# The second weight chunk ahead of the low-rank gate's weights, and a gate product stacked in 96 rows

## The chip, the cores and the metric

The kernel runs on one core of a Trainium2 chip. The metric is the device time of one execution in microseconds (us), as the median of several runs. One core has five engines with a queue each: TensorE (PE, with its weight loads shown as PEld), VectorE (DVE), ScalarE (ACT), GpSimd (POOL) and SyncE (SP), which here only issues transfers. The transfers themselves run on 16 DMA engines.

## The reference

One decoder layer on 256 tokens of 1024 channels in float32: a mixer (gated linear attention beside causal pooling, merged and projected), then a mixture of 64 experts. What matters here is the start of the mixer, where x meets one wide input projection, and the gate of the attention, which has rank 16:

```python
proj = jnp.einsum('bsd,de->bse', x, w_in)          # columns: q 512, k 512, v 1024, r 1024, g_lr 16, u 512, gates 2048
log_decay = jax.nn.log_sigmoid(
    jnp.einsum('bsr,rk->bsk', g_lr, w_gate_up) + b_gate) / GLA_GATE_TEMP     # w_gate_up: 16 x 512
```

## The kernel before, in words

The order of every engine's instructions is the order in which the program writes them (`tc.manual_schedule()`), so an instruction that waits holds all later ones of its engine.

**Precision.** TensorE multiplies float32r data in one pass. To keep float32 accuracy an operand is split in two float32r parts, hi (ACT copies, L295) and lo (DVE subtracts, L296). A product then takes three matmuls: hi by hi, hi by lo, lo by hi (`mm3`, L299 to L301). Plain float32 operands take more passes.

**The input projection.** The weights `w_in` come in chunks of 256 columns, 1 MB each, through a ring of eight buffers that SP fills (`Ring.issue`, L64 to L87). The list `pieces` (L623 to L632) says in which order chunks are worked off: the first chunk of q in four parts with x coming in between, then the gate's piece ("g"), then the second chunk of q in two parts, then k, v and so on. `run` (L305) writes the split of a piece two pieces ahead of its matmuls. After each piece a step of the attention (`gla_steps`, L358) is written in between.

**The low-rank gate.** Its first product is `rank_mm` (L614): 16 matmuls of `wgs` (the hi and lo parts of the 16 columns side by side, 32 columns) with x hi and x lo into `pg`, 32 rows by 256 tokens; ACT copies these to `glr` as float32 (L621). The second product (L362 to L368) multiplies `glr` with `wgu`, in which `w_gate_up` stands twice, one below the other, in plain float32: four matmuls into `plog`. DVE then adds the bias.

**SP's queue at the start** (L256 to L272): x and the first chunk in turns, `wg` (the 16 gate columns), `wgu` as two transfers, `b_gate`, the second chunk (L261), `cst1` (192 KB of constants, L262), the rest of `cst` (L263), five more chunks, then small vectors and the router's weights.

**POOL's queue at the start**: `identb` from `ident` (L278), `trib` from `cst1` (L279), then the zeroing of `A0` and `A1` (L344, L345) and of `B` (L372).

**Later.** After the mixer come the router and 16 rounds of four experts; their matrices stream through rings whose buffers come free when TensorE has used them.

Of the kernel before, what the change touches and what calls it, by code (L numbers as in the profile page):

```python
# [5 lines left out]
FT = mybir.dt.float32  # L6
FR = mybir.dt.float32r
BF = mybir.dt.bfloat16
I32 = mybir.dt.int32
AF = mybir.ActivationFunctionType  # L10
# [3 lines left out]
T, D = 256, 1024  # L14
# [8 lines left out]
NR1, NR2, NR3 = 8, 6, 5  # L23
# [86 lines left out]
def body(ctx, tc, A, out, dbg=lambda *a: None, stop=None):  # L110
    nc = tc.nc
    ctx.enter_context(tc.manual_schedule())
    PE, V, S, G = nc.tensor, nc.vector, nc.scalar, nc.gpsimd
# [74 lines left out]
    ring = Ring(nc, loads)  # L188
# [6 lines left out]
    def bank(tag, shape, name):  # L195
        t = psum.tile([128, 512], FT, name=name, tag=tag, bufs=4)
        n = 1
        for s in shape:
            n *= s
        v = t[:, :n]  # L200
        if len(shape) == 2:
            v = v.rearrange("p (a b) -> p a b", b=shape[1])
        elif len(shape) == 3:
            v = v.rearrange("p (a b c) -> p a b c", b=shape[1], c=shape[2])
        return v
# [23 lines left out]
    ring1 = ctx.enter_context(tc.tile_pool(name="ring1", bufs=NR1))  # L229
# [4 lines left out]
    gla = tc.alloc_tile_pool(name="gla", bufs=1)  # L234
# [8 lines left out]

    x = ring1.tile([128, 2048], FT, name="x", tag="w1", bufs=NR1).rearrange("p (t d) -> p t d", t=2)
    wg = gla.tile([128, 8, 16], FT, name="wg")
    wgu = gla.tile([32, 512], FT, name="wgu")
    wgrp = right.tile([128, 4, 128], FT, name="wgrp")
    nc.scalar.dma_start(ident, A["cst"][:, C_ID:C_ID + 128])
    halves = [slice(0, 512), slice(512, 1024)]
# [5 lines left out]
    ring.between = load_x  # L255
    ring.issue(ring1, "w1", NR1)  # L256
    nc.sync.dma_start(wg, w_in[:, 3072:3088].rearrange("(k p) c -> p k c", p=128))
    for n in range(2):
        nc.sync.dma_start(wgu[16 * n:16 * n + 16], A["w_gate_up"][0])
    nc.sync.dma_start(bgate, A["b_gate"][0].rearrange("(h p) -> p h", p=128))  # L260
    ring.issue(ring1, "w1", NR1)  # L261
    nc.sync.dma_start(cst1, A["cst"][:, C_KEPT:])  # L262
    nc.sync.dma_start(cst[:, C_IOTA:], A["cst"][:, C_IOTA:C_KEPT])  # L263
    ring.open(ring1, "w1", NR1, first=3)
# [6 lines left out]
                                     ap=[[0, 128], [1, E]]))  # L271
# [22 lines left out]
    def split_to(src, hi, lo, eng=V):  # L294
        S.activation(hi, src, AF.Copy)  # L295
        eng.tensor_sub(lo, src, hi.bitcast(FT))  # L296
# [18 lines left out]
    xTh = xt.tile([128, 8, T], FR, name="xTh", tag="xTh", bufs=1)  # L315
    xTl = xt.tile([128, 8, T], FR, name="xTl", tag="xTl", bufs=1)
    def x_part(c):
        p = bank("b", (2, T), "xp")
        for kk in range(2):
            for t in range(2):  # L320
                k = 2 * c + kk
                PE.transpose(p[:, kk, 128 * t:128 * (t + 1)], x[:, t, 128 * k:128 * (k + 1)], ident)
        ks = slice(2 * c, 2 * c + 2)
        split_to(p, xTh[:, ks], xTl[:, ks])


    p = bank("a", (128,), "warm")
# [8 lines left out]

    qT = gla.tile([128, H, T], FT, name="qT")
    kT = gla.tile([128, H, T], FT, name="kT")
    glr = gla.tile([32, T], FT, name="glr")
    wgs = gla.tile([128, 8, 2, 16], FR, name="wgs")  # L340
    v = right.tile([128, 2, D], FT, name="v")
    A0 = right.tile([128, H, 256], FT, name="A0")
    A1 = right.tile([128, H, 128], FT, name="A1")
# [14 lines left out]
    def gla_steps():  # L358
        yield
        xb = gla.tile([128, H, T], FT, name="E", bufs=2)  # L360
        for hp in range(2):
            p = bank("b", (2, T), "plog")  # L362
            for h2 in range(2):
                h = 2 * hp + h2
                PE.matmul(p[:, h2], wgu[:, 128 * h:128 * (h + 1)], glr, start=True, stop=True)
            for h2 in range(2):
                h = 2 * hp + h2
                V.tensor_scalar(xb[:, h], p[:, h2], bgate[:, h:h + 1], None, op0=OP.add)  # L368
# [64 lines left out]
        while m <= 128:  # L433
# [21 lines left out]
            if m < 128:  # L455
                n = H * T // (2 * m)
# [117 lines left out]
    def proj_piece(name, c, part, parts, st):  # L574
        i, kn = li[name, c], 8 // parts

        def sp():
            st[part] = split(ring.get(i)[:, kn * part:kn * (part + 1)], 256 * kn)
            if part == parts - 1:
                ring.done(i)  # L580

        def mm():
            if part == 0:
                st["p"] = bank("a", (2, T), "proj")
            p = st["p"]
            h, l = st[part]
            for j in range(2):
                for kk in range(kn):
                    k = kn * part + kk
                    first, last = k == 0 and j == 0, k == 7  # L590
                    if name == "v":
                        ts = slice(128 * j, 128 * (j + 1))
                        mm3(p[:, j], xTh[:, k, ts], xTl[:, k, ts], h[:, kk], l[:, kk], first, last, True)
                    else:
                        cs = slice(128 * j, 128 * (j + 1))
                        mm3(p[:, j], h[:, kk, cs], l[:, kk, cs], xTh[:, k], xTl[:, k], first, last, True)
            if part < parts - 1:
                return
            cs = slice(2 * c, 2 * c + 2)
            if name == "q":  # L600
                S.activation(qT[:, cs], p, AF.Copy, scale=DK ** -0.5)
            elif name == "k":
                V.tensor_copy(kT[:, cs], p)
            elif name == "v":
                V.tensor_copy(v[:, :, 256 * c:256 * (c + 1)], p)
            elif name == "u":
                V.tensor_copy(uT[:, cs], p)
            elif name == "r":
                S.activation(rT[:, cs], p, AF.Copy)
            else:  # L610
                S.activation(rows(GA if name == "ga" else GB, 2 * c, 2), p, AF.Copy)
        return sp, mm

    def rank_mm():  # L614
        pg = bank("b", (T,), "pg")

        for k in range(8):
            w = wgs[:, k].rearrange("p a r -> p (a r)")
            PE.matmul(pg[:32], w, xTh[:, k], start=k == 0, stop=False)
            PE.matmul(pg[:32], w, xTl[:, k], start=False, stop=k == 7)  # L620
        S.activation(glr, pg[:32], AF.Copy)  # L621

    pieces = []  # L623
    for name, c, _ in chunk_cols:
        st = {}
        parts = 4 if (name, c) == ("q", 0) else 2
        for part in range(parts):
            if parts == 4 and part < 3:
                pieces.append((("x", part, True), lambda: None, lambda part=part: x_part(part + 1)))
            pieces.append(((name, c, part == parts - 1),) + proj_piece(name, c, part, parts, st))  # L630
        if (name, c) == ("q", 0):
            pieces.append((("g", 0, 1), lambda: split_to(wg, wgs[:, :, 0], wgs[:, :, 1]), rank_mm))  # L632

    def done(key):
        finished.add(key)
# [3 lines left out]
    def chain(*gens):  # L639
        for g in gens:  # L640
            yield from g

    finished = {None}
    bgs = [dict(gen=pool_steps(), need=("u", 1)),
           dict(gen=chain(gla_steps(), out_steps(), done("out"), gate_steps()), need=("g", 0))]

    def step_bg():
# [536 lines left out]
    for q in range(NQ):  # L1184
# [34 lines left out]
        if q == SH_UP:  # L1219
            p = bank("b", (2, T), "shu")  # L1220
# [110 lines left out]
```

## Time and profile before

| what | value |
|---|---|
| median of three runs | 690.24 us (690.22 to 690.63) |
| profiled execution, its own time | 690.94 us |
| span of that execution, first to last instruction | 689.1 us |
| mean granted TensorE clock | 0.994 of full speed |

Times in the rows below are in us from the start of the span unless marked ns. An arrow in brackets after a row says how long the engine sat idle before it and what ended that.

### The profile page before, as it was taken

Reading aid. Unit: us, or ns where it says so; the run is one execution under the profiler, and the core shown is the slowest. Engines: PE = TensorE matmul, PEld = TensorE weight load, DVE = VectorE, ACT = ScalarE, POOL = GpSimd, SP = SyncE. Lnnn points to the kernel's source line nnn. Section 1 sums busy time; section 2 is a strip of 40 time slices with the busy share of each in tenths; the row PEclk is TensorE's granted clock in tenths of the full one; section 3 lists DMA queues with packets and bytes.
Section 4 is the critical chain, followed back from the end, with each engine's and each line's share of the span. In section 5 each row is a group of like instructions: output and inputs, shape, how many; then the busy total and the mean of one; then the engine's idle time right before and its main releaser. Section 6 shows DMA issues by size and latency. Waiting matters only on the chain. (4 is left out here: it accounts for less than half of the span.)

```text
span 689.1 us, 13639 instructions
## 1 busy us (share of the span) xinstructions
PE 667.2 (97%) x5928; PEld 472.6 (69%) x5928; DVE 289.3 (42%) x458; ACT 227.9 (33%) x348; POOL 66.2 (10%) x53
## 2 busy tenths in 40 slices
PE   8999999999999999999999999999999999799994
PEld 7999999999999756556556546556655665464632
DVE  4699845946676522122123123333431321231216
ACT  5554546674445213123123113221311311131122
POOL 1063404600002000000000002100000000100001
PEclk9999999999999999999999999999999999999997
DMA  8995533499677999999999999999999999999991
GB/s 265 302 349 185 182 123 126 148 384 421 248 260 300 352 422 384 421 420 418 419 421 419 421 418 416 405 419 421 419 419 421 419 420 420 420 421 416 407 332 63
DMA packets 67429, 242.02 MB, mean 351 GB/s; under 512 B 7044, under 2 KB 37508, under 8 KB 43560
## 3 DMA queue, kind: packets, MB, share of 16 engines
q1 hardware_dynamic: 67224, 241.07, 89.2%
q8 instruction: 47, 0.77, 0.5%
q10 hardware_dynamic: 144, 0.07, 0.1%
q14 instruction: 14, 0.11, 0.0%
HBM read 240.07 MB, written 1.05 MB: 350 GB/s over the span
## 5 line engine op out<-in xcount | busy, mean ns | idle before, releaser
L1032 PE MATMUL pgu<-w,xg 128*64 128x256 f32 x1840 | 222.4, 381 | 1.0 <-DMA w<-in_w_exp_gate 1.0
L1032 PEld LDWEIGHTS pgu<-w,xg 128*64 128x64 f32 x1840 | 140.3, 137 | 84.1 <-ACT Y L1062 11.7
L1057 PE MATMUL py<-w,ht 128*32 128x512 f32 (+1 forms) x912 | 119.3, 580 | 1.9 <-DMA w<-in_w_exp_down 1.5
L296 DVE TENSOR_TENSOR sl<-w,sh 128x1024 fp32r<-128x1024 f32 (+1 forms) x63 | 83.4, 1329 | 42.5 <-ACT sh L295 42.2
L1039 DVE TENSOR_TENSOR h<-sg,pgu 128x256 f32<-128x256 f32 x32 | 13.5, 422 | 192.5 <-ACT sg L1038 146.9
L1063 DVE SCALAR_TENSOR_TENSOR Y<-py,gsl,Y 128x512 fp32r<-128x512 f32 (+1 forms) x66 | 48.5, 735 | 100.5 <-ACT Y L1062 100.4
L1062 ACT ACTIVATE Y<-py,gsl 128x512 fp32r<-128x512 f32 (+1 forms) x66 | 44.5, 675 | 115.1 <-PE py L1057 115.1
L299 PE MATMUL proj<-xTh,sh 128*128 128x256 f32 x288 | 82.2, 285 | 0.0
L301 PE MATMUL proj<-xTh,sl 128*128 128x256 f32 x288 | 80.6, 280 | 0.8 <-DVE sl L296 0.8
L300 PE MATMUL proj<-xTl,sh 128*128 128x256 f32 x288 | 80.6, 280 | 0.0
L1038 ACT ACTIVATE sg<-pgu 128x256 f32<-128x256 f32 x32 | 12.3, 385 | 202.8 <-PE pgu L1032 202.8
L295 ACT ACTIVATE sh<-w 128x1024 fp32r<-128x1024 f32 (+1 forms) x63 | 64.3, 1028 | 34.5 <-PE proj L301 11.0
L1057 PEld LDWEIGHTS py<-w,ht 128*32 128x32 f32 x912 | 30.6, 109 | 54.0 <-issue 45.9
L301 PEld LDWEIGHTS proj<-xTh,sl 128*128 128x128 f32 x288 | 54.0, 187 | 1.3 <-DVE sl L296 1.2
L299 PEld LDWEIGHTS proj<-xTh,sh 128*128 128x128 f32 x288 | 54.1, 188 | 0.8 <-issue 0.3
L300 PEld LDWEIGHTS proj<-xTl,sh 128*128 128x128 f32 x288 | 54.1, 188 | 0.1
L1057 PE MATMUL py<-xTh,ht 128*32 128x512 f32 x80 | 36.3, 594 | 0.0
L1032 PE MATMUL pgu<-xTl,xg 128*64 128x256 f32 x128 | 29.2, 381 | 5.3 <-DMA xTl<-in_w_exp_up 5.3
L785 DVE TENSOR_SCALAR xg<-pgat,cols_sb 128x512 f32<-128x512 f32 x32 | 25.7, 810 | 13.9 <-PE pgat L913 11.5
L913 PE MATMUL pgat<-P,xl 128*128 128x256 f32 x128 | 30.6, 283 | 0.3 <-DVE xl L949 0.3
L787 ACT ACTIVATE xg<-pgat,cols_sb 128x512 f32<-128x512 f32 x32 | 24.7, 778 | 17.2 <-PE pgat L913 17.2
L913 PE MATMUL pgat<-P,xh 128*128 128x256 f32 x128 | 30.3, 283 | 0.0
(271 smaller groups left out, 947.0 us busy)
## 6 DMA issues: line engine op xcount, KB each, us to landing
w<-in_w_exp_gate SPq DMA_DIRECT2D x62, 1024.0 KB, 16.0
w<-in_w_exp_up SPq DMA_DIRECT2D x53, 1024.0 KB, 17.1
w<-in_w_exp_down SPq DMA_DIRECT2D x47, 1024.0 KB, 19.8
w<-in_w_in SPq DMA_DIRECT2D x21, 1024.0 KB, 7.5
xTl<-in_w_exp_up SPq DMA_DIRECT2D x7, 1024.0 KB, 16.2
w<-in_w_exp_down SPq DMA_DIRECT2D x12, 512.0 KB, 15.0
xTh<-in_w_exp_down SPq DMA_DIRECT2D x5, 1024.0 KB, 19.9
w<-in_w_gla_up SPq DMA_DIRECT2D x4, 1024.0 KB, 11.1
```

The costliest lines, as they stand in the source:

```text
L295: S.activation(hi, src, AF.Copy)
L296: eng.tensor_sub(lo, src, hi.bitcast(FT))
L299: PE.matmul(o, ah, bh, start=start, stop=False, skip_group_check=shared_bank)
L300: PE.matmul(o, ah, bl, start=False, stop=False, skip_group_check=shared_bank)
L301: PE.matmul(o, al, bh, start=False, stop=stop, skip_group_check=shared_bank)
L785: V.tensor_scalar(dst, p, g1T[:, k:k + 1], b1T[:, k:k + 1], op0=OP.mult, op1=OP.add)
L787: S.activation(dst, p, AF.Identity, bias=b1T[:, k:k + 1], scale=g1T[:, k:k + 1])
L913: PE.matmul(p[k][:, t].rearrange("p e s -> p (e s)"), part[:, t, k], P8[o][:, t].rearrange("p e s -> p (e s)"), start=part is xh, stop=par ...
L1032: PE.matmul(p[64 * c:64 * c + 64, g], xg[:, k, e].rearrange("p t s -> p (t s)"), w[c][:, k], start=k == 0, stop=k == 7, tile_position=(0, ...
L1057: PE.matmul(p[32 * c:32 * c + 32], HT[2 * q + c // 2][:, j, c % 2, t], ring.get(li["down", 4 * q + c])[:, j, cs], start=j == 0, stop=j == ...
L1062: S.activation(hi, p, AF.Copy, scale=g)
L1063: V.scalar_tensor_tensor(lo, p, g, hi.bitcast(FT), op0=OP.mult, op1=OP.subtract)
```

## The change

The transfer of the second weight chunk is issued right behind `wg`, ahead of the gate's `wgu` and `b_gate`. `wgu` becomes 96 rows (six copies of the 16 rows, one transfer from a repeating address pattern). In `rank_mm` the weights `wgs` stand three times side by side, so that `pg` has 96 rows, of which the first 64 become hi parts and the last 32 lo parts of the product; `wgr` has rows of hi, lo and hi parts of `w_gate_up`. The second product is then one float32r matmul for each head. POOL makes the second and third copy of `wgs`.

```diff
-    wgu = gla.tile([32, 512], FT, name="wgu")
+    wgu = gla.tile([96, 512], FT, name="wgu")
+    wgr = gla.tile([96, 512], FR, name="wgr")
...
     nc.sync.dma_start(wg, w_in[:, 3072:3088].rearrange("(k p) c -> p k c", p=128))
-    for n in range(2):
-        nc.sync.dma_start(wgu[16 * n:16 * n + 16], A["w_gate_up"][0])
+    ring.issue(ring1, "w1", NR1)
+    six = bass.AP(tensor=A["w_gate_up"].tensor, offset=A["w_gate_up"].offset, ap=[[0, 6], [512, 16], [1, 512]])
+    nc.sync.dma_start(wgu, six)
     nc.sync.dma_start(bgate, A["b_gate"][0].rearrange("(h p) -> p h", p=128))
-    ring.issue(ring1, "w1", NR1)
     nc.sync.dma_start(cst1, A["cst"][:, C_KEPT:])
...
-    glr = gla.tile([32, T], FT, name="glr")
-    wgs = gla.tile([128, 8, 2, 16], FR, name="wgs")
+    glr = gla.tile([96, T], FR, name="glr")
+    wgs = gla.tile([128, 8, 3, 2, 16], FR, name="wgs")
...
-                PE.matmul(p[:, h2], wgu[:, 128 * h:128 * (h + 1)], glr, start=True, stop=True)
+                PE.matmul(p[:, h2], wgr[:, 128 * h:128 * (h + 1)], glr, start=True, stop=True)
...
         for k in range(8):
-            w = wgs[:, k].rearrange("p a r -> p (a r)")
-            PE.matmul(pg[:32], w, xTh[:, k], start=k == 0, stop=False)
-            PE.matmul(pg[:32], w, xTl[:, k], start=False, stop=k == 7)
-        S.activation(glr, pg[:32], AF.Copy)
+            w = wgs[:, k].rearrange("p n a r -> p (n a r)")
+            PE.matmul(pg[:96], w, xTh[:, k], start=k == 0, stop=False)
+            PE.matmul(pg[:96], w, xTl[:, k], start=False, stop=k == 7)
+        S.activation(glr, pg[:96], AF.Copy)
+        V.tensor_sub(glr[64:96], pg[64:96], glr[64:96].bitcast(FT))
+        S.activation(wgr, wgu, AF.Copy)
+        V.tensor_sub(wgr[32:64], wgu[32:64], wgr[32:64].bitcast(FT))
+
+    def split_rank():
+        split_to(wg, wgs[:, :, 0, 0], wgs[:, :, 0, 1])
+        G.tensor_copy(wgs[:, :, 1:3], wgs[:, :, 0:1].to_broadcast([128, 8, 2, 2, 16]))
...
-            pieces.append((("g", 0, 1), lambda: split_to(wg, wgs[:, :, 0], wgs[:, :, 1]), rank_mm))
+            pieces.append((("g", 0, 1), split_rank, rank_mm))
```

## Rows read from the trace of the kernel before

**Rows 1.** The page's first part: busy time, share of span and instructions of each engine.

```profile
PE 667.2 (97%) x5928; PEld 472.6 (69%) x5928; DVE 289.3 (42%) x458; ACT 227.9 (33%) x348; POOL 66.2 (10%) x53
```

**Rows 2.** Waits of TensorE from 17 to 410: total, times, longest.

```profile
PE proj L301 <- DVE sl L296: 0.6, 1, 0.6
PE pgat L913 <- DVE xl L949: 0.3, 1, 0.3
```

**Rows 3.** Stretches: busy time by engine, granted clock, DMA share, GB/s.

```profile
60.00:140.00 80.00, 80.00 (x812) 78.66 (x811) 57.79 (x79) 44.89 (x65) 30.44 (x26) 1.00 0.47 152
240.00:410.00 170.00, 168.90 (x1488) 98.46 (x1484) 40.90 (x78) 36.63 (x64) 0.00 (x0) 1.00 1.01 416
```

**Rows 4.** The chain that ended last, around 464: start, us, what.

```profile
464.10 0.01 PE acc L1074
464.12 20.38 DMA w<-in_w_exp_up
```

**Rows 5.** TensorE's timeline, 14 to 17.2: start, duration, instruction.

```profile
14.09 0.28 PE L619 MATMUL pg<-xTh,wgs 128*32 128x256 f32 x1
...
15.93 0.28 PE L299 MATMUL proj<-xTh,sh 128*128 128x256 f32 x1
...
16.91 0.39 PE L301 MATMUL proj<-xTh,sl 128*128 128x256 f32 x1 [0.59 <-DVE sl L296]
```

**Rows 6.** ACT and DVE in the same timeline.

```profile
14.53 1.06 ACT L295 ACTIVATE sh<-w 128x1024 fp32r<-128x1024 f32 x1 [2.54 <-DMA w<-in_w_in]
...
15.63 1.23 DVE L296 TENSOR_TENSOR sl<-w,sh 128x1024 fp32r<-128x1024 f32 x1 [2.79 <-ACT sh L295]
```

**Rows 7.** TensorE's timeline, 19 to 22.5: the gate's second product.

```profile
19.70 1.99 PE L365 MATMUL plog<-glr,wgu 32*128 32x256 f32 x8
21.62 0.39 PE L299 MATMUL proj<-xTh,sh 128*128 128x256 f32 x1
```

**Rows 8.** DVE's timeline: the split of the gate's columns.

```profile
12.56 0.28 DVE L296 TENSOR_TENSOR wgs<-wg,wgs 128x128 fp32r<-128x128 f32 x1
```

**Rows 9.** POOL's timeline, 15 to 18.

```profile
15.08 0.29 POOL L279 CAST trib<-cst 128x128 bf16<-128x128 f32 x1 [10.97 <-DMA cst<-in_cst]
15.31 0.96 POOL L344 MEMSET A<- 128x1024 f32 x1
16.20 0.53 POOL L345 MEMSET A<- 128x512 f32 x1
16.67 0.96 POOL L372 MEMSET B<- 128x1024 f32 x1
```

**Rows 10.** POOL's groups by form: busy, mean ns, idle before.

```profile
L918 POOL CAST xh<-x 128x1024 fp32r<-128x1024 f32 x1 | 2.1, 2150 | 72.4 <-PE mix L301 72.4
```

**Rows 11.** SP's queue, 5 to 11: start, duration of the issue.

```profile
5.50 3.00 SPq L259 DMA_DIRECT2D wgu<-in_w_gate_up  x2
...
9.00 0.51 SPq L83 DMA_DIRECT2D w<-in_w_in  x1
9.56 1.01 SPq L262 DMA_DIRECT2D cst<-in_cst  x1
```

**Rows 12.** Stretches from 9 to 13, columns as in rows 3.

```profile
9.00:9.75 0.75, 0.75 (x9) 0.75 (x8) 0.00 (x0) 0.46 (x1) 0.00 (x0) 1.00 0.79 138
9.75:10.50 0.75, 0.75 (x8) 0.75 (x8) 0.58 (x1) 0.66 (x2) 0.00 (x0) 1.00 0.55 46
10.50:11.25 0.75, 0.75 (x8) 0.64 (x6) 0.71 (x2) 0.57 (x2) 0.00 (x0) 1.00 0.75 183
...
12.00:13.00 1.00, 1.00 (x10) 0.93 (x9) 0.84 (x3) 0.00 (x0) 0.00 (x0) 1.00 1.07 357
```

**Rows 13.** Stretches at the end of the span, columns as in rows 3.

```profile
679.00:680.00 1.00, 0.52 (x2) 0.32 (x2) 0.96 (x4) 0.94 (x2) 0.00 (x0) 1.00 0.00 0
...
680.50:681.00 0.50, 0.00 (x0) 0.00 (x0) 0.50 (x1) 0.00 (x0) 0.50 (x1) 0.79 0.00 0
681.00:682.00 1.00, 0.00 (x0) 0.00 (x0) 0.97 (x3) 0.29 (x1) 0.92 (x2) 0.50 0.00 0
```

**Rows 14.** TensorE's timeline at the start of the span.

```profile
1.15 3.38 PE L331 MATMUL warm<-onesb 128*128 128x128 bf16 x30 [1.15 <-DVE ones L277]
...
6.57 0.38 PE L299 MATMUL proj<-xTh,sh 128*128 128x256 f32 x1
```

## Prediction

> **What bounds the kernel now.** I read the page's first part, then TensorE's waits, then busy times by stretch, then the chain that ended last, and only then the first 25 us, where the change lies. TensorE is busy for 97% of the span [rows 1]. From 17 to 410 us it waits 0.9 us in all [rows 2], so from the first chunks on it sets the pace. The transfers do not: from 60 to 140 us the DMA engines are busy 0.47 of the time, because a ring buffer must come free first; from 240 us on they are full as well, at 416 GB/s [rows 3]. At 464 us the chain passes from TensorE to the expert transfers, which then set the end [rows 4]. Both halves hang on TensorE's early pace: the full stream of transfers begins only when TensorE has released the buffers of the mixer. A microsecond that TensorE gains or loses near 15 us therefore shifts everything behind it by about one microsecond. I count it in full, against the profiled execution's 690.94 us (span 689.1) and the median of 690.24 alike; the two differ by 0.7 us, so the sum is given as a difference and added to the median.
>
> **What the change removes.** First, a stall. The first product of the gate begins at 14.09 and its 16 matmuls end in the next piece's first at 15.93, 1.84 us, 0.115 each. That piece, the second chunk's first half, starts two matmuls and then stands until 16.91 for its lo part [rows 5], because the chunk landed at 14.53 and ACT's 1.06 us and DVE's 1.23 us come after it [rows 6]. At 0.115 a matmul the piece would have begun at 16.68 to run on without a gap, so 16.68 − 15.93 = 0.75 us is what an early enough chunk gives back. Its issue moves from 9.00 to 5.50 [rows 11]; SP may hold it there, as it holds the two `wgu` issues for 3.00 us now. The DMA engines stand partly idle from 9.00 to 11.25: shares 0.79, 0.55 and 0.75 of 0.75 us each leave 0.16 + 0.34 + 0.19 = 0.69 us [rows 12]. Filling that brings the chunk to 13.8, its lo part to about 15.2. The 0.75 us are then gone, but only if the gate's product is not itself late.
>
> Second, passes. The second product takes from 19.70 to 21.62, 1.92 us, as plain float32 [rows 7]. Four float32r matmuls of 256 columns at the 0.115 of rows 5 take 0.46. That saves 1.46 us of TensorE. The three-fold stack costs nothing in the first product: 16 matmuls of the same 256 columns, with a wider weight load that overlaps them, as the 128-column loads of the projection do.
>
> **What it adds that lies beside other work.** ACT's copy of `glr` stays one instruction; ACT's copy of `wgu` (96 by 512) and DVE's two subtractions (32 by 256 and 32 by 512) are each below the 1.06 and 1.23 us of a 128 by 1024 operation [rows 6], some 0.6 and 1.1 us. They come between the two products, and the 24 matmuls of the chunk's first half lie there, 24 x 0.115 = 2.8 us. Behind them in the queues are the splits of the third chunk, which TensorE needs two pieces later, 5.6 us. I cost them at nothing; without that cover it would be 1.7 us.
>
> **What it adds on the path.** The first product now also waits for POOL's copy of `wgs`, and POOL works in written order. Its inputs are ready at 12.84 (DVE's 12.56 + 0.28) [rows 8]. But ahead of it in POOL's queue stands `trib`, which waits for `cst1` until 15.08, and behind that the zeroing of `A0` and `A1`; the instruction after these starts at 16.67, 1.59 us after `cst1` [rows 9]. The new copy takes that place. So the piece that was meant to run at 14.1 starts only when `cst1` has landed, plus 1.59, plus the copy.
>
> *When `cst1` lands.* It lands now 0.55 us behind the chunk (14.53 and 15.08). In the changed order the chunk, `wgu` and `b_gate` are all still ahead of it. `wgu` grows from 64 to 192 KB; 128 KB more at 357 GB/s [rows 12] are 0.37 us. Lower end: all idle time is filled, 15.08 − 0.69 + 0.37 = 14.76. Upper end: none is, 15.45. I take 15.1.
>
> *The copy.* 512 elements in a partition, not seen in the trace. Below, POOL's zeroing of 512 elements, 0.53 us [rows 9]; above, half of its cast of 1024 elements to float32r, 1.08 [rows 10], whose source is strided. The copy reads and writes short contiguous runs, nearer to the first: 0.7.
>
> *Sum.* The first matmul starts at 15.1 + 1.59 + 0.7 + 0.2 (signal and one weight load, 96 columns; 0.1 to 0.3) = 17.6 instead of 14.09. The next piece starts at 17.6 + 1.84 = 19.4, against the gapless 16.68 now: 2.75 us lost, the 0.75 included. Less 1.46 saved in the second product: +1.3 us. With both ends of both costs, +0.75 to +2.0.
>
> *The clock.* TensorE would stand still for 3.5 us. The trace has one such place, the end: TensorE was busy for 0.52 of 679 to 680, with its last two matmuls; the granted clock, still 1.00 then, was 0.79 in 680.5 to 681 and 0.50, the 1.2 GHz level, from 681 on [rows 13]. [...] I expect it to fall here too. What it takes to come back is seen at the start: 30 matmuls of 128 columns in 3.38 us, 0.11 each, are the pace of 1.2 GHz, and at 6.57, when the projection begins, the pace is 2.4 GHz's 0.115 for 256 [rows 5, 14]. That is 3.4 to 5.4 us of work at half speed, half of it lost: at most 2.7 us, at least nothing if the clock holds or comes back within the stall. As part of the slow time may lie in the stall, I take 1.3. Total +2.6 us: **692.8 us**.
>
> **A rule that speaks against it too.** The rows above treat `wgu` as spread over all 16 DMA engines. The Trainium skill, DMA: Bandwidth & Descriptors, section "Why a DMA increments its semaphore by 16 and not by 1", says that a transfer is split over the largest number up to 16 that divides the slowest dimension of both sides; here these are 6 copies and 96 rows, so 6 engines. No row shows which engines a transfer uses. By that rule six engines carry 32 KB each, `cst1` comes later than by the even sum, and the time is that of rival 1, 693.7 instead of 692.8 us.
>
> **The rivals.**
> 1. *`cst1` later still.* If `wgu` runs on few engines, say six, its 192 KB take 192/(357 x 6/16) = 1.5 us there instead of 0.55, and `cst1` lands at about 16.0. The stall grows to 4.4 us, which makes the clock's fall surer: +3.5, 693.7 us. For it: the repeating source pattern is unlike any transfer of the trace. Against: nothing there shows an uneven spread. This is what the Trainium skill's rule above would do.
> 2. *The stall without the clock's fall.* +1.3 us, 691.5 (691.0 to 692.2). For it: the 0.75 us gap at 16 left the clock at 1.00, as did all waits of the middle. Against: this one is more than four times as long, and the end of the span.
> 3. *Faster.* TensorE does not wait for POOL, because the copy runs ahead of the `cst1` wait: then both savings stand, −0.75 − 1.46 = −2.2, 688.0 us. The point that decides is the time at which `cst1` lands: with the clock up, the change breaks even at 15.1 − 1.3 = 13.8, and the whole gain needs 11.6. Against: 1 MB of chunk stands ahead of it in SP's queue and lands at 13.8 itself; POOL waited 10.97 us at exactly that place.
> 4. *It does not reach the end.* The full transfer stream from 240 us on absorbs it: 690.2. Against: that stream is started by TensorE's progress.
>
> **How the numbers follow.** Forecast (even spread, clock falls) 0.32; rival 1, 0.25; rival 2, 0.28; rival 3, 0.10; rival 4, 0.05. The likeliest is 692.8; its own range is 691.6 to 694.0. The range to 690.8 below and 694.6 above takes in rivals 1 and 2 but for their edges and leaves out rivals 3 and 4 and some 0.04 above. A change of 0.2% (1.4 us), about what a measurement of this kernel can tell from none, means 688.9 or 691.6. Slower: 0.31 + 0.25 + 0.12 of rival 2 = 0.68. Same: 0.16 of rival 2, 0.05 of rival 4, 0.01 of the forecast = 0.22. Faster: 0.10.
>
> **What would show it.** In the changed profile TensorE waits for POOL ahead of L619's successor by about 3.5 us, POOL's copy starts 1.6 us after `trib`, and `trib` still waits for `cst1` until about 15. The wait for the second chunk's lo part is gone. The second product takes 0.5 us. The granted clock is 0.50 for some microseconds near 18. No wait or a short one on POOL makes the forecast wrong, and so does a clock of 1.00 throughout.

## The result, and the profile after

The kernel became slower: median 694.34 us (693.32 to 695.16, 6 runs) against 690.56 (690.22 to 691.85, 6 runs) beside it, a ratio of 1.0055, 95% interval 1.0044 to 1.0067. The forecast was 692.8 with a range of 690.8 to 694.6. The profiled execution took 694.33 us, its span 692.6, against 690.94 and 689.1: 3.4 to 3.5 us more.

The first part of the page shows nothing of it, and that is the first lesson: TensorE's busy time even went down (667.2 in [rows 1]).

```profile
PE 666.1 (96%) x5924; PEld 472.1 (68%) x5924; DVE 289.0 (42%) x460; ACT 228.5 (33%) x349; POOL 68.7 (10%) x54
```

The waits of TensorE from 17 to 410 us show it at once. In [rows 2] the longest was 0.6 us; now one wait for POOL stands there (columns: total, times, longest).

```profile
PE pg L621 <- POOL wgs L630: 4.8, 1, 4.8
PE pgat L922 <- DVE xl L958: 0.3, 1, 0.3
```

What POOL did meanwhile, in its timeline (start, duration, instruction, in brackets the idle time before it and what ended it); compare [rows 9]:

```profile
16.32 0.41 POOL L280 CAST trib<-cst 128x128 bf16<-128x128 f32 x1 [12.44 <-DMA cst<-in_cst]
16.68 0.95 POOL L345 MEMSET A<- 128x1024 f32 x1
17.56 0.52 POOL L346 MEMSET A<- 128x512 f32 x1
18.04 0.61 POOL L630 CAST wgs<-wgs 128x512 fp32r<-128x512 f32 x1
```

POOL waited for `cst1`, made `trib`, zeroed `A0` and `A1`, and only then made the copy for which TensorE stood. TensorE's timeline, to be held against [rows 5] and [rows 7]:

```profile
18.70 0.53 PE L621 MATMUL pg<-xTh,wgs 128*96 128x256 f32 x1 [4.84 <-POOL wgs L630]
19.02 0.41 PE L622 MATMUL pg<-xTl,wgs 128*96 128x256 f32 x1
...
21.88 0.28 PE L622 MATMUL pg<-xTl,wgs 128*96 128x256 f32 x1
22.00 0.28 PE L300 MATMUL proj<-xTh,sh 128*128 128x256 f32 x1
...
24.83 0.64 PE L366 MATMUL plog<-glr,wgr 96*128 96x256 f32 x4
25.30 0.28 PE L300 MATMUL proj<-xTh,sh 128*128 128x256 f32 x1
```

The first product starts at 18.70 instead of 14.09 and takes 22.00 − 18.70 = 3.30 us instead of 1.84. The clock is down meanwhile, as the stretches show (length, then busy us and instructions of TensorE, its weight loads, DVE, ACT and POOL, then the granted clock, the DMA share and GB/s):

```profile
13.00:14.00 1.00, 0.86 (x8) 0.66 (x6) 0.00 (x0) 0.00 (x0) 0.00 (x0) 1.00 1.10 219
14.00:15.00 1.00, 0.00 (x0) 0.00 (x0) 0.00 (x0) 0.73 (x1) 0.00 (x0) 1.00 1.13 222
...
18.00:19.00 1.00, 0.30 (x1) 0.30 (x2) 0.01 (x1) 0.00 (x0) 1.00 (x3) 0.65 1.09 348
19.00:20.00 1.00, 1.00 (x6) 1.00 (x6) 0.00 (x0) 0.00 (x0) 0.54 (x1) 0.50 1.11 349
...
21.00:22.00 1.00, 1.00 (x7) 1.00 (x7) 0.00 (x0) 0.00 (x0) 0.00 (x0) 0.64 1.10 346
22.00:23.00 1.00, 1.00 (x11) 1.00 (x10) 0.39 (x1) 0.80 (x2) 0.00 (x0) 1.00 1.10 348
```

Clock 1.00 is the 2.4 GHz level and 0.50 the 1.2 GHz one: six or seven matmuls end in a microsecond while it is low, eleven in the last row. Then the gate's second product needs 25.30 − 24.83 = 0.47 us where [rows 7] had 1.92, so that saving is real. What follows it starts at 25.30 instead of 21.62, 3.68 us later, and this stays to the end: the chain of waits goes over from TensorE to the expert transfers at 467.52 instead of 464.12 [rows 4], 3.40 later.

```profile
467.52 19.83 DMA w<-in_w_exp_up
```

SP's queue and the two engines that split the second chunk, against [rows 11] and [rows 6], in their timelines:

```profile
5.44 1.84 SPq L83 DMA_DIRECT2D w<-in_w_in  x1
7.32 2.14 SPq L261 DMA_DIRECT2D wgu<-in_w_gate_up  x1
...
10.08 0.49 SPq L263 DMA_DIRECT2D cst<-in_cst  x1
```

```profile
14.27 1.06 ACT L296 ACTIVATE sh<-w 128x1024 fp32r<-128x1024 f32 x1 [2.59 <-DMA w<-in_w_in]
...
15.36 1.22 DVE L297 TENSOR_TENSOR sl<-w,sh 128x1024 fp32r<-128x1024 f32 x1 [2.96 <-ACT sh L296]
```

The chunk is issued 3.56 us earlier (5.44 and 9.00) and lands 0.26 us earlier (14.27 and 14.53). That is no more than landings scatter: the same order of transfers had it land at 14.03 to 14.54 in four more profiles below, the order of before at 14.41 in one.

### The profile page after: what moved, and what is told of

Same layout as the page of the kernel before. It is cut to its first block, busy times and chain, and to the rows that moved or that the text cites. A ratio compares the mean times of both kernels' runs of the same rounds, so it can differ in the third digit from the quotient of the medians.

```text
span 692.6 us, 13634 instructions
## 1 busy us (share of the span) xinstructions
PE 666.1 (96%) x5924; PEld 472.1 (68%) x5924; DVE 289.0 (42%) x460; ACT 228.5 (33%) x349; POOL 68.7 (10%) x54
## 3 DMA queue, kind: packets, MB, share of 16 engines
HBM read 240.21 MB, written 1.05 MB: 348 GB/s over the span
## 5 line engine op out<-in xcount | busy, mean ns | idle before, releaser
L297 DVE TENSOR_TENSOR sl<-w,sh 128x1024 fp32r<-128x1024 f32 (+1 forms) x63 | 81.0, 1291 | 40.5 <-ACT sh L296 40.3
```

## The experiments

Each was timed against the kernel before on the same chip; intervals are 95%. Diffs are against the changed kernel unless another is named. "Lead" and "loss" are the start of an instruction against the same one of the kernel before.

**Which part makes the loss.** The two parts were run one by one: the new order alone, as an edit of the kernel before, and the stack alone, with `wgu` and `b_gate` ahead of the chunk again.

```
     nc.sync.dma_start(wg, w_in[:, 3072:3088].rearrange("(k p) c -> p k c", p=128))
+    ring.issue(ring1, "w1", NR1)
     for n in range(2):
         nc.sync.dma_start(wgu[16 * n:16 * n + 16], A["w_gate_up"][0])
     nc.sync.dma_start(bgate, A["b_gate"][0].rearrange("(h p) -> p h", p=128))
-    ring.issue(ring1, "w1", NR1)
```

> The kernel before with only the second chunk's transfer moved ahead of wgu and b_gate. If the chunk's arrival decides, it lands some 0.3 to 0.7 us earlier, the 0.87 us gap ahead of the third matmul of the second chunk shrinks by as much, and the time falls by up to 0.5 us to about 690.2. If what comes next, the third chunk and the chain of VectorE and ScalarE behind it, takes the lead back before 38 us, the time stays that of the kernel before. POOL is not in the path either way, so it is not slower.

Order alone: 690.21 us against 690.39, ratio 0.9996 (0.9987 to 1.0005), no difference. The stall on the second chunk shrank, as TensorE's timeline shows, but did not go:

```profile
16.60 0.39 PE L301 MATMUL proj<-xTh,sl 128*128 128x256 f32 x1 [0.22 <-DVE sl L296]
```

The idle time before it was 0.59 in [rows 5]. The chunk landed at 14.21.

```
-    ring.issue(ring1, "w1", NR1)
     nc.sync.dma_start(wgu, six)
     nc.sync.dma_start(bgate, A["b_gate"][0].rearrange("(h p) -> p h", p=128))
+    ring.issue(ring1, "w1", NR1)
```

> The changed kernel with the transfers in the order of before (wgu and b_gate ahead of the second chunk). If POOL's place behind trib and cst1 is the cause, the wait for POOL is there all the same, some 3.5 to 5 us, and the time is near that of the changed kernel, 693.5 to 694.5 us. If the new order of the transfers made cst1 late, the wait shrinks below 3 us and the time is below 692.5.

Stack alone: 694.17 against 690.39, 1.0058 (1.0045 to 1.0072), the whole loss. POOL and TensorE in its timeline:

```profile
15.95 0.29 POOL L280 CAST trib<-cst 128x128 bf16<-128x128 f32 x1 [12.04 <-DMA cst<-in_cst]
...
17.54 0.63 POOL L630 CAST wgs<-wgs 128x512 fp32r<-128x512 f32 x1
...
18.23 0.53 PE L621 MATMUL pg<-xTh,wgs 128*96 128x256 f32 x1 [4.31 <-POOL wgs L630]
```

So the wait comes from the stack, not from the chunk standing ahead of `cst1`. The larger `wgu` alone moves `cst1` from 15.08 to 15.95, 0.87 us for 128 KB more; in one more profile with these transfers (the stack with a fill, below) `cst1` came at 16.29, 1.21 us later than before.

**Is it POOL's queue?** Two kernels keep the stack and take that wait away: one lets ACT and DVE write all three copies of `wgs`, so that no POOL copy is there; the other leaves the copy on POOL but puts `trib` behind it.

```
-        split_to(wg, wgs[:, :, 0, 0], wgs[:, :, 0, 1])
-        G.tensor_copy(wgs[:, :, 1:3], wgs[:, :, 0:1].to_broadcast([128, 8, 2, 2, 16]))
+        w3 = wg[:, :, None, :].to_broadcast([128, 8, 3, 16])
+        split_to(w3, wgs[:, :, :, 0], wgs[:, :, :, 1])
```

> The three copies of wgs are written by ACT and DVE from a broadcast source, so POOL makes none. If POOL's place in the path is the cause (it stands behind trib, which waits for cst1), TensorE starts the first product near 14 us without a wait, the clock stays at 1.00, the chunk's lo part is still some 0.4 us late (the chunk landed at 14.27), the second product keeps its 1.45 us: about 1.9 us below the kernel before, 688.7 us, where the changed kernel has 694.3. If the rows of 96 or the order of the transfers cost the time, it stays above 692.

690.87 against 690.78, 1.0005 (0.9995 to 1.0014). The whole loss is gone, and so is the gain that was expected in its place. TensorE's timeline of this kernel:

```profile
13.87 0.28 PE L621 MATMUL pg<-xTh,wgs 128*96 128x256 f32 x1
...
19.60 0.71 PE L366 MATMUL plog<-glr,wgr 96*128 96x256 f32 x4
20.15 0.28 PE L300 MATMUL proj<-xTh,sh 128*128 128x256 f32 x1
...
32.29 0.39 PE L302 MATMUL proj<-xTh,sl 128*128 128x256 f32 x1 [0.32 <-DVE sl L297]
...
37.99 0.88 PE L391 MATMUL gs<-qT,kT 128*32 128x32 f32 x64
```

Behind the second product it leads by 21.62 − 20.15 = 1.47 us; at the first `gs` matmul (38.68 before) by 0.69. In between TensorE waits until 32.29 for a lo part that DVE makes.

```
-    G.tensor_copy(trib, cst_of(C_TRI, 128))
...
     def split_rank():
         split_to(wg, wgs[:, :, 0, 0], wgs[:, :, 0, 1])
         G.tensor_copy(wgs[:, :, 1:3], wgs[:, :, 0:1].to_broadcast([128, 8, 2, 2, 16]))
+        G.tensor_copy(trib, cst_of(C_TRI, 128))
```

> POOL's copy stays, only trib's cast is written behind it. If the wait of trib for cst1 is the cause, POOL zeroes A0 and A1 before 6 us, copies wgs near 12.4 to 13.1 us, and the time is that of the kernel without the copy, 688.7 us. If the copy itself is slow or late for another reason, TensorE still waits for POOL for over 1 us and the time stays above 691.

691.34 against 690.78, 1.0007 (0.9998 to 1.0017). POOL now makes the copy while it would have waited:

```profile
12.80 0.61 POOL L629 CAST wgs<-wgs 128x512 fp32r<-128x512 f32 x1 [7.53 <-DVE wgs L296]
16.75 1.19 POOL L630 CAST trib<-cst 128x128 bf16<-128x128 f32 x1 [3.34 <-DMA cst<-in_cst]
```

The first product starts at 14.03 and the matmul behind the second at 19.64, 1.98 us ahead of before; the first `gs` starts at 38.58, 0.1 ahead: TensorE waited for lo parts until 29.47 (0.76 us) and 32.88 (0.32). One line's place in POOL's written order decides some 3 us; that the loss is POOL's order is shown by both kernels. That a gain reaches the end is refuted by both.

**What the clock costs.** Matmuls on constants fill the stall, so that the clock stays up.

```
     def rank_mm():
         pg = bank("b", (T,), "pg")
+        warm(76)
```

> 76 extra bf16 matmuls of 128 columns fill most of the wait before the first product (some 4.3 us of 4.8). If the fall of the clock costs what the changed profile shows (first product 3.3 instead of 1.84 us), the clock stays at 1.00 and the time falls by 1.4 us to about 692.9 us. If the clock's fall is made up later or the fill delays the product, it stays at 694.3 us or above.

694.55 against 690.78, 1.0048 (1.0034 to 1.0062). The clock is 1.00 from 5 to 26 us, and TensorE's timeline shows what that is worth there:

```profile
13.93 4.42 PE L332 MATMUL warm<-onesb 128*128 128x128 bf16 x76
18.85 0.36 PE L622 MATMUL pg<-xTh,wgs 128*96 128x256 f32 x1 [0.50 <-POOL wgs L631]
...
20.82 0.28 PE L300 MATMUL proj<-xTh,sh 128*128 128x256 f32 x1
...
24.12 0.28 PE L300 MATMUL proj<-xTh,sh 128*128 128x256 f32 x1
```

The product takes 1.97 us instead of 3.30, and the matmul behind the second product starts 25.30 − 24.12 = 1.18 us earlier than in the changed kernel. It still leads by 1.18 us at the first `gs` matmul (41.08 and 42.26). At the end this is not seen: by the two ratios, 1.0048 and 1.0055, the fill is worth 0.5 us, less than either interval is wide. The same fill was tried on the stack alone, to see it a second time.

> The stacked product with the transfers in the order of before, with 76 extra bf16 matmuls in the wait for POOL: a second look at what the fall of the clock costs. If the slow clock's cost reaches the end, the clock stays at 1.00, the first product takes 1.9 instead of 3.2 us and the time is 1.2 us below that of the same kernel without the fill, 693.0 us instead of 694.2. If a lead of that size is lost again later, as in the first fill, it stays near 694.2.

693.54 against 690.43, 1.0049 (1.0035 to 1.0063), where the stack alone had 1.0058. Its first `gs` matmul starts at 40.7 instead of 41.8. So the clock's fall costs 1.1 to 1.2 us at 25 to 40 us, shown twice. The profiles show where most of it goes. At 540 us the first fill still starts its expert matmuls 0.77 us ahead of the changed kernel, and then stands until an expert matrix has landed, the first two rows; the changed kernel, in the two below them, does not wait there:

```profile
539.60 4.10 PE L1042 MATMUL pgu<-w,xg 128*64 128x256 f32 x34
544.00 0.43 PE L1042 MATMUL pgu<-xTl,xg 128*64 128x256 f32 x1 [0.29 <-DMA xTl<-in_w_exp_up]
540.37 3.88 PE L1041 MATMUL pgu<-w,xg 128*64 128x256 f32 x33
543.88 0.38 PE L1041 MATMUL pgu<-xTl,xg 128*64 128x256 f32 x1
```

The fill on the stack alone loses 0.8 us at the same place, with a wait of 0.17 us for the same transfer at 543.01. How much of the 1.1 to 1.2 us is left in the time, these few runs do not settle.

**Is a delay passed on in full?** The kernel before, with 60 such matmuls ahead of the first product.

```
     def rank_mm():
         pg = bank("b", (T,), "pg")
+        warm(60)
```

> The kernel before with 60 extra bf16 matmuls of 128 columns (some 3.4 us of TensorE) ahead of the gate's first product and nothing else. TensorE's later work starts 3.4 us later, 0.75 of it in place of the wait for the second chunk: 2.65 us net. If a loss at 14 us passes to the end in full, the time rises by 2.6 us to about 693.2. If the same slack that swallows a lead swallows part of a loss, by 1.9 us, to 692.5; if the stream of expert transfers absorbs it, by less than 1 us.

692.55 against 690.39, 1.0031 (1.0019 to 1.0044), 2.2 us by the medians. In TensorE's timeline:

```profile
14.07 3.52 PE L331 MATMUL warm<-onesb 128*128 128x128 bf16 x60
...
24.00 0.38 PE L299 MATMUL proj<-xTh,sh 128*128 128x256 f32 x1
```

24.00 − 21.62 = 2.38 us lost there, 1.9 at the first `gs`, 2.2 at the end. Losses pass on, less some tenths.

**Why is `cst1` late?** The source pattern of `wgu` was turned: its slowest dimension is then 16 rows instead of 6 copies.

```
-    ap=[[0, 6], [512, 16], [1, 512]]
+    ap=[[512, 16], [0, 6], [1, 512]]
```

> The source pattern of wgu has its 16 rows as the slowest dimension and the six copies inside, the same bytes in one transfer; the rows land in another order, so the gate's values are not the reference's. If the slowest dimension of six confined wgu to few DMA engines and made cst1 late, cst1 now lands at about 15.2 instead of 16.3 us, the wait for POOL falls from 4.8 to about 3.7 us and the time to about 693.2 us. If wgu was spread evenly anyway, cst1 stays near 16.3 and the time near 694.3 us.

695.38 against 690.78, 1.0066 (1.0053 to 1.008), no better. `cst1` did come earlier, but POOL got nothing from it, as its timeline and DVE's show:

```profile
15.66 1.24 POOL L280 CAST trib<-cst 128x128 bf16<-128x128 f32 x1 [11.82 <-DMA cst<-in_cst]
...
15.53 1.23 DVE L297 TENSOR_TENSOR sl<-w,sh 128x1024 fp32r<-128x1024 f32 x1 [2.81 <-ACT sh L296]
```

`trib` starts 0.66 us before that of the changed kernel, and 0.5 us before the earliest of the four profiles with the change's own transfers (16.16, 16.32, 16.57 and 16.75, which is how far `cst1` scatters). It lasts 1.24 us instead of 0.41, until DVE's subtraction ends (16.76). POOL's copy starts at 18.21. The clock also fell earlier here, to 0.55 already in 16 to 17 us. An earlier `cst1`, seen once, speaks for the uneven spread; the time says nothing on it.

**Where the gain goes.** In the kernels without the wait, TensorE leads at 20 us and has lost it by 38. The chain there goes from the third chunk: ACT splits it, DVE subtracts and adds the biases, ACT takes the Exp and what follows it, then splits the fourth chunk. If that chain sets the end, bringing the third chunk in earlier must bring the lead. It was put ahead of `b_gate` and the constants, first with `wgu` in six transfers of 16 rows, to spread that transfer. Both this kernel and the two behind it build on the one without POOL's copy.

```
-    nc.sync.dma_start(wgu, six)
+    for n in range(6):
+        nc.sync.dma_start(wgu[16 * n:16 * n + 16], A["w_gate_up"][0])
+    ring.issue(ring1, "w1", NR1)
     nc.sync.dma_start(bgate, A["b_gate"][0].rearrange("(h p) -> p h", p=128))
...
-    ring.open(ring1, "w1", NR1, first=3)
+    ring.open(ring1, "w1", NR1, first=4)
```

> The kernel with the three copies written by ACT and DVE, the six copies of wgu as six transfers, and the third chunk's transfer also ahead of b_gate and cst1. If the lead of 1.5 to 2 us that TensorE had at 20 us was lost because the third chunk landed at 19.3 to 19.8 us and ScalarE and VectorE followed from there, the third chunk now lands by about 18, the lead holds past 38 us and the time is 1 us below the kernel before, about 689.5. If the lead is lost to the two engines' own work, or to something later, it stays at 690.5 to 691.

690.29 against 690.39, 0.9997 (0.9988 to 1.0006). The test failed in its means, as SP's queue shows:

```profile
7.99 4.74 SPq L261 DMA_DIRECT2D wgu<-in_w_gate_up  x6
12.78 0.42 SPq L83 DMA_DIRECT2D w<-in_w_in  x1
```

The third chunk could only be issued at 12.78 and landed at 19.38. With the one transfer of the change kept (the same edit without its first three lines):

> No copy on POOL (ACT and DVE write the three copies), wgu as one transfer, and the third chunk's transfer ahead of b_gate and the constants. In four profiles the first scores of the attention (gs) begin 12.43 us after ScalarE's Exp, and that begins 6.2 to 6.3 us after the split of the third chunk, which begins when the chunk lands (19.2 to 19.9). If that chain is what swallowed TensorE's lead, the chunk lands by about 18.5, gs begins as much earlier, near 37.3 instead of 38.0 to 38.7, and the time falls by about 1 us against the kernel before, to 689.4. If gs stays at 38 or the end does not follow, the time stays at 690.3 to 690.8.

690.11 against 690.43, 0.9998 (0.9989 to 1.0007). The third chunk landed at 19.00, 0.63 us earlier than before, and not by 18.5. ACT and TensorE in its timeline, and behind them the same three rows of the kernel before:

```profile
19.00 2.01 ACT L297 ACTIVATE sh<-w 128x1024 fp32r<-128x1024 f32 x2 [1.03 <-DMA w<-in_w_in]
...
25.31 1.06 ACT L377 ACTIVATE F<-F 128x1024 f32<-128x1024 f32 x1 [1.38 <-DVE F L376]
...
37.74 0.88 PE L392 MATMUL gs<-qT,kT 128*32 128x32 f32 x64
```

```profile
19.63 2.00 ACT L295 ACTIVATE sh<-w 128x1024 fp32r<-128x1024 f32 x2 [2.35 <-DMA w<-in_w_in]
25.82 1.06 ACT L375 ACTIVATE F<-F 128x1024 f32<-128x1024 f32 x1 [0.47 <-DVE F L374]
38.68 0.76 PE L390 MATMUL gs<-qT,kT 128*32 128x32 f32 x64
```

Here are the three starts (split of the third chunk on ACT, Exp, first `gs`) in the kernels so far that don't wait for POOL, without the delayed one:

```
                     split    Exp     gs     Exp - split   gs - Exp
before               19.63   25.82   38.68      6.19        12.86
order alone          19.94   26.13   38.56      6.19        12.43
no POOL copy         19.25   25.56   37.99      6.31        12.43
trib behind          19.84   26.15   38.58      6.31        12.43
six transfers        19.38   25.70   38.13      6.32        12.43
third chunk ahead    19.00   25.31   37.74      6.31        12.43
```

In the last five the first `gs` stands 12.43 us behind the Exp to a hundredth, whatever TensorE's lead was at 20 us (0.31 us with the order alone, 0.82 to 1.98 in the four with the stack). Only in the kernel before it comes later, by 0.43: there TensorE itself was still the last, as it waits for nothing behind the stall of [rows 5] in [rows 2]. So a lead of TensorE is cut down to what the third chunk's arrival leaves, 0.1 to 0.9 us. The end shows none of that within these measurements, whose intervals are some 0.6 us to either side. In the profiles a part of it goes behind 38 us: the lead of 0.94 us with the third chunk ahead is 0.43 at the `gs` group at 77 us (76.31 and 76.74), and the 0.12 with the order alone has turned into 0.38 behind (77.12). TensorE shows no wait there and its clock is 1.00, so the same matmuls took a little longer; no run shows why. One more way to bring the third chunk in early is to take `wgu` off SP's queue, on top of the edit before: ACT issues it, behind the split of x's first part.

```
-    nc.sync.dma_start(wgu, six)
...
+    nc.scalar.dma_start(wgu, six)
```

> As the one before, with wgu issued from ScalarE's queue after its first copy, so that SP is not held by it. If SP's issue of wgu delays the chunks, the second lands by 14 and the third by 18 us, and the time is 1 to 1.5 us below the kernel before, 689 us. If the bytes and not the issue delay them, or if the transfer takes bandwidth from the first chunk's last parts, it is no better than the one before.

690.45 against 690.43, 1.0000 (0.9991 to 1.0009). The second chunk landed only at 16.48 and the first product began at 15.44. The first `gs` again stands 12.44 us behind the Exp (39.08 and 26.64), 0.4 us later than before, and the time is that of before: the order of the queues changed which piece waits, not the end.

## Why the prediction held, and what was mis-sized

The mechanism came as forecast, step by step: POOL's copy behind `trib` and the two memsets, TensorE's stall, the clock's fall, the shorter second product. Only sizes were off: 694.34 lies above the range that the prediction gave its own forecast (691.6 to 694.0) and inside the stated one, which also covers rival 1. What it cost at nothing, the added work of ACT and DVE, stayed at nothing: the 24 matmuls between the products take 2.83 us (22.00 to 24.83) and no wait follows them. On TensorE's path, up to the matmul behind the second product:

```
term                              forecast   measured
first product later                +3.5       +4.61   (18.70 - 14.09)
clock                              +1.3       +1.46   (3.30 - 1.84)
gap in the second chunk gone       -0.75      -0.94   (19.70 - 15.93 less 24.83 - 22.00)
second product shorter             -1.46      -1.45   (1.92 - 0.47)
sum                                +2.6       +3.68   (25.30 - 21.62)
```

Against the fill, where the same product starts after a wait with the clock up, the clock's term is 3.30 − 1.97 = 1.33 us, the forecast's 1.3.

**The mis-sized term is when `cst1` lands:** `trib` starts at 16.32 where 15.1 was taken, 1.2 us later, which is more than the 1.1 that the sum lacks. The upper end (15.45) was too low as well. The prediction gave the transfer of 128 KB more the mean rate, 0.37 us, and took 0.69 us of idle DMA time as fillable by an earlier issue. The DMA engines' idle time from 9.00 to 11.25 did fill (shares of 1.05 to 1.33), but the chunk landed no earlier than landings scatter. Measured apart, the larger `wgu` costs 0.87 and 1.21 us (the two profiles of the stack alone), the earlier chunk alone 0.09 (`trib` at 15.17, order alone); both together 1.08 to 1.67 (16.16 to 16.75). So most of it is the larger `wgu`, at two to three times the 0.37 us of the mean rate. SP held the chunk's issue for 1.84 us and `wgu`'s for 2.14, and the DMA engines moved 219 to 222 GB/s from 13 to 15 us at a busy share above 1. The prediction knew that SP might hold the issue but put no price on it; the chunk landed at 14.27 where 13.8 was said.

**Rival 1** named that size, 16.0 and 693.7 us, with the uneven spread of `wgu` as its cause. The size stands. The cause is supported and not settled: with the pattern turned, `cst1` came 0.66 us earlier, in one profile. The rule of the Trainium skill, DMA: Bandwidth & Descriptors, section "Why a DMA increments its semaphore by 16 and not by 1", fits both numbers; but no view shows which engines a transfer used, and the rate fell in the turned kernel too (171 GB/s from 13 to 14 us), and with the order alone, where `wgu` is as before (203).

**POOL's steps:** from `trib` to the copy 1.72 us instead of 1.59, as `trib` took 0.41 us for 0.29; the copy 0.61 for 0.7; to the first matmul 0.05 for 0.2.

**The clock** fell, so rival 2 is out; 1.46 us were lost on TensorE for 1.3, of which 1.33 are the clock's. That the size came out has some luck in it: it was a middle between nothing and 2.7 us, taken from the pace of the first matmuls of the span, where the view gives a granted clock of 1.00.

**Rivals 3 and 4.** The price of 688.0 us in rival 3 was wrong. With POOL's wait gone TensorE led by 1.47 and 1.98 us at 20 us, from the second product in both kernels and from the gap in the second chunk only with `trib` behind, by 0.52 us (without POOL's copy the chunk landed at 14.54 and the gap stayed). The time was that of before. The failed premise stands in the first part: a microsecond that TensorE gains or loses near 15 us shifts everything behind it. It holds for a loss (3.68 us there, 3.4 to 3.8 at the end; 2.38 there, 2.2 at the end) and not for a gain, because the third chunk's chain through ACT and DVE ends 0.43 us ahead of TensorE in the kernel before. TensorE's 97% of the span hid a second limit that near. The chain is read from the fixed 12.43 us and from TensorE's waits for DVE; that no other limit follows was not tried, and the fills' wait at 544 us is one. Rival 4 looked for that absorption in the full stream from 240 us on. For the kernels without POOL's wait it sits at 20 to 38 us and in part up to 77; the two fills lost 0.8 to 0.9 us in that stream; and the loss of the changed kernel passed through both.

## What to carry to other kernels

Before work is given to an idle engine, read what stands ahead of it in that engine's written order, and what that waits for: POOL was idle nine tenths of the time, and its one wait for a late constant made a copy of 0.6 us cost TensorE 4.6. Price a loss and a gain apart: a loss on the engine that sets the pace passes on, but here a gain only reached as far as the next chain behind it, which is found by the distance of fixed pairs of instructions over several kernels. A transfer moved ahead in a queue is worth what its landing moves, here 0.26 us for 3.56 us of earlier issue, and one profile does not tell such a shift from scatter.

## What the runs showed of the hardware

**POOL's cast is held by DVE's subtraction.** The cast to `trib` takes 0.29 us alone (before, stack alone). Where it starts during DVE's 128 by 1024 subtraction it ends just behind that: 16.73 after 16.58 in the changed kernel, 16.90 after 16.76 with the pattern turned, 17.94 after 17.78 with `trib` behind (1.19 us instead of 0.29). POOL's memset keeps its 0.95 us beside the next subtraction. The Trainium skill, SBUF — State Buffer, section "Who interferes with whom", says that a VectorE instruction with two inputs in SBUF contends with a GpSimd instruction that reads SBUF and not with one that only writes it; these numbers agree with it. That is why the turned pattern's earlier `cst1` brought POOL nothing.

**The clock falls at different times in like stalls.** TensorE's last matmul before the stall starts at 13.58 in the changed kernel and the clock falls in 18 to 19 us; with the stack alone it falls in 17 to 18 (0.92), and with the pattern turned, in a stall of about the same length, it is at 0.55 already in 16 to 17. The fill of 76 matmuls kept it at 1.00.

**Issues took SP long.** One issue of `wgu` took SP 2.14 us, six smaller ones of the same data 4.74, and the 1 MB chunk ahead of it 1.84 and 2.41, where the chunk's issue took 0.51 in [rows 11]. What SP waits for in them no view shows.
